# Two input rows per partition moved from Pool's load to SyncE's load at the start of a mixture-of-experts kernel

## The chip, the cores and the metric

The kernel runs on one core of one Trainium2 chip. The metric is device time in microseconds (us) of that core for one execution. The kernel before takes 180.09 us, the median of three runs (179.96 to 180.34).

A core has five instruction streams that concern us: TensorE (PE in the profile, its weight loads PEld), VectorE (DVE), ScalarE (ACT), GpSimd (POOL, called Pool here) and SyncE (SP). Loads and stores between the chip's memory (HBM) and the on-chip memory (SBUF) are carried by 16 DMA engines. A transfer is issued by Pool or by SyncE, is cut into packets, and is spread over all 16 DMA engines. In the profile q0 is the queue of what Pool issues and q1 of what SyncE issues. Only what Pool issues changes the type of the numbers on the way here (float32 in HBM to bfloat16 in SBUF); SyncE's load keeps float32.

## What is computed

```python
n_experts, capacity, hidden, expert_hidden = 8, 256, 512, 2048
# x  (8, 256, 512)   w1 (8, 512, 2048)   w2 (8, 2048, 512), all float32
h = np.matmul(x, w1)
h = np.maximum(h, 0)
return np.matmul(h, w2).astype(np.float32)
```

For each of eight experts, 256 tokens go through two matrix products with a ReLU between. x has 4 MB, the weights 64 MB together, the output 4 MB.

## The kernel before

**Memory.** All places in SBUF are given by hand. `w1_sb` and `w2_sb` have four slots (NS), one expert each, in bfloat16. `hT` holds the hidden layer of one expert, `xT` the transposed x of all experts, `out_sb` the output of all experts in float32. Two of these places have a second use at the start: `x_sb`, the x in bfloat16, is slot 2 of `w2_sb` (line 73), and `x_head`, the float32 copy of the first rows of x, lies in the places of the first experts of `out_sb` (line 134).

**x.** The 2,048 rows of x are laid out as 128 partitions of R = 16 rows with 512 numbers each; a partition's 16 rows lie side by side in HBM (`x_v`, line 49). The first HEAD rows of each partition are loaded by SyncE in float32 into `x_head` (line 136), before the two calls that close the setup (lines 138 and 139), and VectorE casts them into `x_sb` (line 215) once they have landed (semaphore `d_head`). The rest is loaded and cast on the way by Pool (line 154), as its first instruction after the setup. TensorE's transposes (line 329) wait for the cast (`s_cast`), for the identity matrix that Pool makes (lines 155 to 166), and for Pool's load (`d_pool`). They take four rounds of 16; VectorE and ScalarE copy the results from PSUM to `xT` (line 207).

**Weights.** Pool issues all weight loads (line 191), in the order of the list `loads` (lines 119 to 125): w1 of experts 0 and 1, w2 of the same two, then w1 and w2 of 2 and 3, then 4 and 5, then one expert at a time, the last w2 in two halves. The first three are issued without a wait, right after the identity. The w2 load of experts 2 and 3 waits for the transposes, since it overwrites `x_sb`; the later ones wait until the expert that had the slot before is done. SyncE waits for each load's landing and passes it on to TensorE as a count (line 144).

**Experts.** TensorE runs a loop of eight experts. For each, 64 matmuls (two halves of 32, a loop of its own) make the hidden layer in `h_ps`; ScalarE applies the ReLU and writes `hT` (line 240). Then 32 matmuls make the output in `o_ps`, which VectorE copies to `out_sb` (line 226), and ScalarE for the very last half expert (line 246).

**Stores.** Pool stores experts 0 to 6 in one transfer (line 194), issued behind all loads; SyncE stores expert 7 (line 146) when its copies are done. A tiny store ahead of the last weight load (line 182) takes part in the order of the two.

Of the kernel before, what the change touches and what calls it, by code (L numbers as in the profile page):

```python
# [16 lines left out]
def kernel(  # L17
# [14 lines left out]

    R = E * C // P

    HEAD = 4

    NS = 4

# [94 lines left out]

    x_head = out_sb[:, :HEAD // MC].rearrange("p e m h -> p (e m h)")

    head = nc.sync.dma_start(x_head, x_v[:, :HEAD * H]).then_inc(d_head, 16)
    tc.info.no_tile_sem_insts.add(head.ins.name)
# [15 lines left out]
    pool = nc.gpsimd  # L153
    pool.dma_start(x_sb[:, HEAD * H:], x_v[:, HEAD * H:]).then_inc(d_pool, 16)  # L154
    pool.memset(identity[:], 0.0).then_inc(s_event)  # L155
# [58 lines left out]
    dve.wait_ge(d_head, 16)  # L214
    dve.tensor_copy(x_sb[:, :HEAD * H], x_head).then_inc(s_cast)  # L215
    dve.sem_inc(c_xt[0], 1)
# [259 lines left out]
```

## Time and profile before

| | |
|---|---|
| median of three runs | 180.09 us |
| the profiled execution's own time | 179.48 us |
| its span, first to last instruction | 178.2 us |
| mean granted TensorE clock, share of full speed | 0.939 |
| DMA packets, bytes written | 3744, 40.37 MB |
| SyncE's load of the head of x, issue at 0.74 us | 1024 KB, 4.7 us to landing |
| Pool's load of the rest of x, issue at 2.41 us | 1536 KB (as written), 10.8 us to landing |

All figures but the first come from one profiled execution; the profile's own times count from the start of its span. Bytes of a DMA are counted as they are written: a load that turns float32 into bfloat16 reads twice what is counted, so 212 GB/s of it is 424 GB/s of HBM reads. "Share" of a DMA queue is the time of its packets over the time of 16 DMA engines, so in a stretch of T us with n packets the mean packet took share x 16 x T / n; packets are picked by their start, so the share of a short stretch can be far over 100%. In the DMA line of the page a digit is the busy share of a fortieth of the span in tenths. Rows of a timeline read: start, duration, engine, line, operation, written tile <- read tile, and in brackets how long the engine had been idle and what released it.

### The profile page before, as it was taken

Reading aid. Unit: us, or ns where it says so; the run is one execution under the profiler, and the core shown is the slowest. Engines: PE = TensorE matmul, PEld = TensorE weight load, DVE = VectorE, ACT = ScalarE, POOL = GpSimd, SP = SyncE. Lnnn points to the kernel's source line nnn. Section 1 sums busy time; section 2 is a strip of 40 time slices with the busy share of each in tenths; the row PEclk is TensorE's granted clock in tenths of the full one; section 3 lists DMA queues with packets and bytes.
Section 4 is the critical chain, followed back from the end, with each engine's and each line's share of the span. In section 5 each row is a group of like instructions: output and inputs, shape, how many; then the busy total and the mean of one; then the engine's idle time right before and its main releaser. Section 6 shows DMA issues by size and latency. Waiting matters only on the chain. (4 is left out here: it accounts for less than half of the span.)

```text
span 178.2 us, 2068 instructions
## 1 busy us (share of the span) xinstructions
PE 128.2 (72%) x824; PEld 90.4 (51%) x832; DVE 15.8 (9%) x20; ACT 38.7 (22%) x38; POOL 10.9 (6%) x21
## 2 busy tenths in 40 slices
PE   0007620694029999996059999999999999949991
PEld 0006520593013596495024794695696597438740
DVE  0203420000000110020000200200200110020001
ACT  2002420044000044045000152062044044004401
POOL 4500010000000002011000101100020000001000
PEclk9999999999755999999858999999999999996998
DMA  6999999999999999999999999999999999999997
GB/s 208 240 203 232 224 202 221 224 217 206 228 217 202 232 217 199 232 221 195 232 224 195 232 224 199 224 224 202 221 224 217 206 228 213 206 206 221 294 424 326
DMA packets 3744, 40.37 MB, mean 227 GB/s; under 512 B 288, under 2 KB 288, under 8 KB 1312
## 3 DMA queue, kind: packets, MB, share of 16 engines
q0 software_dynamic: 3456, 38.80, 97.7%
q1 hardware_dynamic: 288, 1.57, 2.4%
HBM read 71.30 MB, written 4.20 MB: 424 GB/s over the span
## 5 line engine op out<-in xcount | busy, mean ns | idle before, releaser
L276 PE MATMUL o_ps<-w_sb,hT 128*128 x248 | 60.5, 399 | 18.7 <-PEq L99 17.9
L276 PE MATMUL h_ps<-xT,w_sb 128*128 x512 | 61.8, 284 | 11.5 <-PEq L99 11.5
L276 PEld LDWEIGHTS h_ps<-xT,w_sb 128*128 x512 | 58.3, 146 | 15.9 <-issue 12.2
L240 ACT ACTIVATE hT<-h_ps 128x1024 bf16<-128x1024 f32 x32 | 32.8, 1024 | 111.1 <-PE h_ps L276 111.1
L276 PEld LDWEIGHTS o_ps<-w_sb,hT 128*128 128x128 bf16 x256 | 25.5, 102 | 50.9 <-issue 24.7
L226 DVE COPY out_sb<-o_ps 128x512 f32<-128x512 f32 x15 | 9.7, 687 | 141.2 <-PE o_ps L276 141.2
L276 PE MATMUL xt_ps<-identity,w_sb 128*128 128x128 bf16 x64 | 7.6, 310 | 15.9 <-PEq L99 15.9
L276 PEld LDWEIGHTS xt_ps<-identity,w_sb 128*128 x64 | 6.5, 145 | 16.7 <-issue 16.7
L191 POOL DMA_DIRECT2D w_sb<-in_w_dram x12 | 8.1, 673 | 103.5 <-PE h_ps L276 57.8
L207 ACT COPY xT<-xt_ps 128x1024 bf16<-128x1024 bf16 x4 | 4.0, 1012 | 17.2 <-PE xt_ps L276 17.2
L207 DVE COPY xT<-xt_ps 128x1024 bf16<-128x1024 bf16 x4 | 4.9, 1225 | 12.3 <-PE xt_ps L276 12.3
L194 POOL DMA_DIRECT2D out_dram<-out_sb x1 | 1.0, 964 | 33.5 <-DMA out_dram<-out_sb 33.5
L246 ACT COPY out_sb<-o_ps 128x512 f32<-128x512 f32 x1 | 0.6, 586 | 5.9 <-PE o_ps L276 5.9
L207 ACT ACT_TABLE_LOAD x1 | 1.3, 1283 | 2.0 <-PEq L139 2.0
L215 DVE CAST w_sb<-out_sb 128x2048 bf16<-128x2048 f32 x1 | 1.2, 1227 | 5.5 <-DMA out_sb<-in_x_dram 5.5
L182 POOL DMA_DIRECT2D out_dram<-out_sb x1 | 0.5, 512 | 14.7 <-DVEq L229 14.7
L154 POOL DMA_DIRECT2D w_sb<-in_x_dram x1 | 0.7, 682 | 2.0 <-POOLq L139 2.0
L158 POOL TENSOR_SCALAR_AFFINE_SELECT identity<-identity 128x128 bf16<-128x128 bf16 x1 | 0.3, 284 | 0.2 <-POOL identity L155 0.2
L155 POOL MEMSET identity<- 128x128 bf16 x1 | 0.2, 224 | 0.0
L460 POOL MEMSET const-float32-0.0<- 128x1 f32 x1 | 0.1, 94 | 0.2 <-issue 0.2
L460 POOL MEMSET const-bfloat16-1.0<- 128x1 bf16 x1 | 0.1, 97 | 0.0
L460 POOL MEMSET const-uint8-127<- 128x1 uint8 x1 | 0.1, 97 | 0.0
(1 smaller groups left out, 0.1 us busy)
## 6 DMA issues: line engine op xcount, KB each, us to landing
w_sb<-in_w_dram POOLq DMA_DIRECT2D x5, 4096.0 KB, 47.1
w_sb<-in_w_dram POOLq DMA_DIRECT2D x5, 2048.0 KB, 51.1
out_dram<-out_sb POOLq DMA_DIRECT2D x1, 3584.0 KB, 12.9
w_sb<-in_w_dram POOLq DMA_DIRECT2D x2, 1024.0 KB, 43.6
w_sb<-in_x_dram POOLq DMA_DIRECT2D x1, 1536.0 KB, 10.8
out_sb<-in_x_dram SPq DMA_DIRECT2D x1, 1024.0 KB, 4.7
out_dram<-out_sb SPq DMA_DIRECT2D x1, 512.0 KB, 3.1
out_dram<-out_sb POOLq DMA_DIRECT2D x1, 1.0 KB, 33.9
```

The lines of the kernel that those rows point to most:

```text
L154: pool.dma_start(x_sb[:, HEAD * H:], x_v[:, HEAD * H:]).then_inc(d_pool, 16)
L158: pool.affine_select(out=identity[:], in_=identity[:], compare_op=mybir.AluOpType.not_equal, fill=1.0, base=0, pattern=[[-1, P]], channel_ ...
L182: pool.dma_start(out_v[:16, 0, :16], out_sb[:16, 0, 0, :16]).then_inc(d_pool, 16)
L191: pool.dma_start(dst, src).then_inc(landed[i][0], 16)
L194: pool.dma_start(out_v[:, :E - 1, :], out_sb[:, :E - 1].rearrange("p e m h -> p e (m h)")).then_inc(d_pool, 16)
L207: return copy(xT[:, ko, m].rearrange("k (ep r2) -> k ep r2", r2=R // MC), xt_ps[m][:].rearrange("k r2 ep -> k ep r2"),)
L215: dve.tensor_copy(x_sb[:, :HEAD * H], x_head).then_inc(s_cast)
L226: cp = dve.tensor_copy(out_sb[:, e, m, :], o_ps[m][:])
L240: act.activation(hT[:, g * GJ:(g + 1) * GJ, :].rearrange("p a c -> p (a c)"), h_ps[g % UG][:], mybir.ActivationFunctionType.Relu,).then_in ...
L246: act.copy(out_sb[:, E - 1, 1, :], o_ps[1][:]).then_inc(v_last)
L276: return pe.add_instruction(inst)
L460: nc = _bacc.Bacc("TRN2", target_bir_lowering=False, num_devices=1)
```

## The change

SyncE's load takes six of the sixteen rows of each partition instead of four, Pool's takes ten instead of twelve. `HEAD` appears in the shape of `x_head` (two experts' places of `out_sb` become three), in both loads, and in VectorE's cast of the head, which becomes 128 x 3072 instead of 128 x 2048. No instruction is added, removed or moved in any engine's stream.

```diff
@@ -32,7 +32,7 @@
 
     R = E * C // P
 
-    HEAD = 4
+    HEAD = 6
 
     NS = 4
 
```

The lines that use it, unchanged:

```python
x_head = out_sb[:, :HEAD // MC].rearrange("p e m h -> p (e m h)")
head = nc.sync.dma_start(x_head, x_v[:, :HEAD * H]).then_inc(d_head, 16)
...
pool.dma_start(x_sb[:, HEAD * H:], x_v[:, HEAD * H:]).then_inc(d_pool, 16)
...
dve.tensor_copy(x_sb[:, :HEAD * H], x_head).then_inc(s_cast)
```

## The prediction

> **What bounds the kernel now.** I read the page's DMA lines first, then the chain of waits, then the waits of SyncE's queue.
>
> ```profile
> PE 128.2 (72%) x824; PEld 90.4 (51%) x832; DVE 15.8 (9%) x20; ACT 38.7 (22%) x38; POOL 10.9 (6%) x21
> DMA  6999999999999999999999999999999999999997
> q0 software_dynamic: 3456, 38.80, 97.7%
> q1 hardware_dynamic: 288, 1.57, 2.4%
> HBM read 71.30 MB, written 4.20 MB: 424 GB/s over the span
> ```
>
> The 16 DMA engines are full from the first slice to the last; TensorE is busy 72% and waits for weights. q0 is Pool's queue, q1 SyncE's. The chain that ended last agrees, once its start is asked about:
>
> ```profile
> 158.49 0.04 issue
> 158.53 8.85 PE h_ps L276 x64
> ...
> 174.37 0.59 ACT out_sb L246
> ```
> ```profile
> SPq L144 <- DMA w_sb<-in_w_dram: 166.0, 12, 30.7
> ```
>
> SyncE waits 166.0 us for weights. The chain starts at 158.53, when the last expert's w1 has landed, and runs on TensorE to the last store. That store does not find the DMA engines idle either (by stretches: length, busy time of PE, PEld, DVE, ACT, POOL, clock, DMA share, GB/s):
>
> ```profile
> 172.00:174.00 2.00, 2.00 (x11) 0.87 (x9) 0.00 (x0) 0.00 (x0) 0.00 (x0) 1.00 1.02 422
> 174.00:176.00 2.00, 0.34 (x2) 0.00 (x0) 0.69 (x1) 0.59 (x1) 0.00 (x0) 1.00 1.01 414
> 177.00:178.20 1.20, 0.00 (x0) 0.00 (x0) 0.00 (x0) 0.00 (x0) 0.00 (x0) 0.50 0.18 72
> ```
>
> So the end is the end of a packet stream that has no holes. Each DMA engine carries its own sixteenth of every load, and a load has landed when the last engine is through. The next four rows are the DMA view by the start of packets (queue: packets, MB, time of these packets as a share of 16 engines over the stretch), for 20 to 140 us, 7.5 to 12 us, 12.095 to 12.100 and 12.911 to 12.915:
>
> ```profile
> q0 software_dynamic: 1713, 25.97, 101.4%
> ...
> q0 software_dynamic: 80, 0.98, 103.0%
> ...
> q0 software_dynamic: 1, 0.02, 1532.5%
> ...
> q0 software_dynamic: 1, 0.02, 1915.6%
> ```
>
> First row: 1.014 x 16 x 120 / 1713 = 1.136 us for 15.16 kB, which is 1.228 us for a weight packet of 16,384 B; a single one (third row) took 15.325 x 16 x 0.005 = 1.226 us. For 120 us, then, no packet was slow, whatever the engines did. The third and fourth rows are the first weight packet on the quickest and on the slowest DMA engine: 12.10 and 12.91. With equal work and no slow packets behind, these 0.8 us must still stand when the last w1 lands. **What the slowest DMA engine loses before 12.9 us is paid at the end of the kernel, one for one; nothing else in the first 13 us is.** That is where the change works.
>
> **The change part by part.** The stretch before 13 us, from the timeline:
>
> ```profile
> 0.74 0.38 SPq L136 DMA_DIRECT2D out_sb<-in_x_dram  x1
> 2.41 0.68 POOL L154 DMA_DIRECT2D w_sb<-in_x_dram  x1 [1.96 <-POOLq L139]
> 3.99 2.85 POOL L191 DMA_DIRECT2D w_sb<-in_w_dram  x3 [0.15 <-issue]
> 5.46 1.23 DVE L215 CAST w_sb<-out_sb 128x2048 bf16<-128x2048 f32 x1 [5.46 <-DMA out_sb<-in_x_dram]
> 13.73 1.89 PE L276 MATMUL xt_ps<-identity,w_sb 128*128 128x128 bf16 x16 [13.73 <-PEq L99]
> ```
>
> *The bytes.* From 3.25 to 4.60 only the head moves:
>
> ```profile
> q1 hardware_dynamic: 70, 0.57, 100.2%
> ```
>
> That is 1.002 x 16 x 1.35 / 70 = 0.309 us for a head packet of 8,192 B. A packet of Pool's x load (24,576 B read, 12,288 written) took 1.030 x 16 x 4.5 / 80 = 0.927 us between 7.5 and 12. Per byte read both are 0.0377 us/kB. Each DMA engine has 8 of each. After: 8 head packets of 12,288 B at 0.309 x 1.5 = 0.464, and 8 of Pool's reading 20,480 B at 0.927 x 5/6 = 0.772. Before 8 x (0.309 + 0.927) = 9.89 us, after 8 x (0.464 + 0.772) = 9.89. Moving rows between the queues is worth 0.00 by itself: 1.24 us more head, 1.24 us less rest.
>
> *The cast L215.* 1.23 x 1.5 = 1.84 us, starting 1.24 us later, at 6.7, done by 8.5. Its reader is PE at 13.73, which also waits for the whole of x. Cost nothing, with 5 us of cover; beyond that the transposes would be late, whose result is first used when the first weight load has landed, 28.5 us after its issue at 3.99 (next rows). TensorE's, ScalarE's and SyncE's other work is the same.
>
> *SyncE's and Pool's issues.* One instruction each, as before, for 128 rows:
>
> ```profile
> w_sb<-in_x_dram POOLq DMA_DIRECT2D x1, 1536.0 KB, 10.8
> out_sb<-in_x_dram SPq DMA_DIRECT2D x1, 1024.0 KB, 4.7
> ```
>
> x is complete at 2.41 + 10.8 = 13.2, the head at 5.4. Pool's three weight issues follow: 2.85 us in all, minimum, median and maximum (ns), and the times from issue to landing, in the view of this line for that stretch:
>
> ```profile
> L191 POOL DMA_DIRECT2D w_sb<-in_w_dram x3: 733/748/1383, 4.0 to 5.4; - x3
> ...
> DMA to landing us min/median/max: 28.5/47.1/65.8
> ```
>
> The 1383 is the third, from 5.45, and the cast stands over it from 5.46 to 6.69; the first two took 733 and 748. After the change the cast starts at 6.7, when three issues of 0.74 from 3.99 are over (6.2). Pool would gain 0.64 us, but the third load stands behind the second, which lands at 4.73 + 47.1 = 51.8: worth nothing through Pool's own order.
>
> The Trainium skill (SBUF — State Buffer, "SBUF: two separate sides") says that a VectorE fp32 copy from SBUF to SBUF holds a port that GpSimd needs to write descriptors, and that the DMA engines then wait for these. The long third issue agrees; by this rule the sum would be 0 if x's own descriptors had been written by 5.46, and a gain of the kind worked out next if not.
>
> *The take-over from head to rest.* Here is the one loss that the change can touch. Pool's packets that start between 4.62 and 7.5:
>
> ```profile
> q0 software_dynamic: 48, 0.59, 102.6%
> ```
>
> 1.026 x 16 x 2.88 / 48 = 0.985 us, against 0.927 afterwards: 0.058 x 3 packets = 0.17 us lost on an average engine. On the slowest one it is more. Its first two packets start at 5.104 and 6.276 (asked for in the stretches 5.104 to 5.105 and 6.276 to 6.277); six normal ones follow, up to 12.9:
>
> ```profile
> q0 software_dynamic: 1, 0.01, 7443.8%
> ...
> q0 software_dynamic: 1, 0.01, 7450.0%
> ```
>
> They took 74.438 x 16 x 0.001 = 1.191 and 1.192 us: 2 x 0.265 = **0.53 us lost**. These slow packets lie where Pool issues (3.99 to 6.84) and where the cast runs (5.46 to 6.69). No head packet between 3.25 and 4.6 was slow, although Pool was issuing from 3.99. After the change that stretch carries head packets until 5.86 to 6.34, and Pool's first packets meet at most the last 0.3 us of Pool's issuing. Bounds: all of it goes, -0.53; nothing goes, 0; with the cast as its cause it grows, +0.26 to +0.53 (below). I take -0.45, nearer to the first, since the row of head packets is clean beside the same issuing.
>
> *The start.* Packets started from 1.70 to 3.25, and the first two of the slowest engine (from 1.855 to 1.865 and from 2.390 to 2.395):
>
> ```profile
> q1 hardware_dynamic: 49, 0.40, 93.4%
> ...
> q1 hardware_dynamic: 1, 0.01, 331.9%
> ...
> q1 hardware_dynamic: 1, 0.01, 710.0%
> ```
>
> Mean 0.934 x 16 x 1.55 / 49 = 0.473 us against 0.309; the two took 0.531 and 0.568, so 0.48 lost. If this is a slow stretch of time, the larger packets lose the same: 0. If each early packet takes longer in proportion, 1.5 x 0.48 = 0.72: +0.24. I take 0, because full speed is there by 3.25 on all engines, which began up to 0.7 us apart.
>
> Sum: 0.00 (bytes) + 0 (cast) + 0 (issues) - 0.45 (take-over) + 0 (start) = -0.45 us. The profiled execution took 179.48 us, its span 178.2 and 1.3 around it, 0.61 below the median 180.09. Taken off the profiled 179.48 that gives 179.03; as a difference it holds for the median too: **179.65 us**, own range 179.45 to 179.9. About 0.36 us (0.2%) is what a measurement of this kernel can tell from no change.
>
> **The rivals.**
>
> *Nothing changes (180.1).* The slow packets belong to the beginning of Pool's queue, whenever that is; then they move 1.24 us later with it. For: they are the first and second of Pool's. Against: most engines' first Pool packet was not slow (average loss 0.17, slowest 0.53). It also comes out so if Pool's packets now alternate with the head's: the same bytes on the same engines; the head then lands later, within the cast's 5 us. The Trainium skill (DMA: Bandwidth & Descriptors, "Issuing engines are not separate DMA queues") says that transfers of all issuers run on the same 16 engines, so spreading them saves issue time only; the equal 0.0377 us/kB agree, and by that rule alone it is this case.
>
> *Slower: the cast is what slows Pool's packets (180.35 to 180.6).* Place: L215, now 1.84 us long and over Pool's packets from beginning to end, where the old one met two per engine. Price: 0.265 us for each packet touched. 1.84 us over packets of 0.77 touch three or four: 3 x 0.265 - 0.53 = +0.26, or 4 x 0.265 - 0.53 = +0.53. It decides from four packets on the slowest engine. For: the two slow packets (5.10 to 7.47) enclose the cast. Against: the row for 20 to 140 us has VectorE copying beside unslowed packets, though from PSUM.
>
> *Slower start (180.1 + 0.24 = 180.33)*, as worked out above, with the take-over's loss unchanged. For: two early packets in a row were slow. Against: from 3.25 on no head packet is slow on any engine.
>
> *The change doesn't do what it says:* the issue row of either load would still show 1024 and 1536 KB. An edit of two row counts leaves no room for it; no chance given.
>
> **How the numbers follow.** Take-over loss gone: 0.50 (0.40 beyond 0.36 us, 0.10 within). Nothing changes: 0.20 (0.02 faster, 0.16 within, 0.02 slower). Cast: 0.20 (0.02 within, 0.18 slower, being the higher price or the lower with some of the start's). Start: 0.10 (0.06 within, 0.04 slower). So faster 0.42, same 0.34, slower 0.24. The range runs from all of the 0.53 gone and a little jitter (179.45) to the cast's upper price (180.65).
>
> **What would show it.** Bytes: SyncE's head 1536 KB, landing near 6.6; Pool's rest 1280 KB, x complete near 12.7 instead of 13.2. Cast: about 1.84 us from 6.7. Issues: three at L191 of about 0.75 us each. Take-over: the mean Pool packet from 5.9 to 8.5 at 0.77 us, not 0.80 or more, and the last engine's first weight packet at 12.4. PE's start on the last expert and the span then come 0.4 to 0.5 us earlier. Wrong: slow packets under the new cast (12.91 rises to 13.2), slow ones at the start of Pool's queue again (12.91 stays), or an end that does not follow the first weight packet of the slowest engine.

## The result and the profile after

| | before | after |
|---|---|---|
| median of six runs each | 179.95 us | 179.25 us |
| lowest to highest | 179.68 to 180.34 | 179.17 to 179.49 |
| ratio after / before, 95% interval | | 0.9961 [0.9948, 0.9974] |
| profiled execution, its own time / span | 179.48 / 178.2 us | 179.49 / 178.2 us |

The change makes the kernel 0.70 us faster, which is more than the predicted 0.45 and below the predicted range. Yet the two profiled executions are equally long. Both statements are true, and the second one is where a reader of a single profile goes wrong here.

The timeline and the issue rows of the kernel after, beside those shown of before:

```profile
3.98 2.19 POOL L191 DMA_DIRECT2D w_sb<-in_w_dram  x3 [0.15 <-issue]
7.21 1.76 DVE L215 CAST w_sb<-out_sb 128x3072 bf16<-128x3072 f32 x1 [7.21 <-DMA out_sb<-in_x_dram]
```
```profile
out_sb<-in_x_dram SPq DMA_DIRECT2D x1, 1536.0 KB, 6.4
w_sb<-in_x_dram POOLq DMA_DIRECT2D x1, 1280.0 KB, 10.8
```

The bytes moved as the diff says; Pool's three issues take 0.66 us less than before (2.19 for 2.85), since the cast no longer stands over the third. But the head lands at 0.74 + 6.4 = 7.1 us and x is complete at 2.40 + 10.8 = 13.2, where the prediction had 6.6 and 12.7; the reason follows. Now the DMA view of the kernel after by the start of packets (queue: packets, MB, share of 16 engines), for 5.9 to 8.5 us, for 2.015 to 2.016, and for 12.931 to 12.932:

```profile
q0 software_dynamic: 54, 0.55, 101.5%
q1 hardware_dynamic: 21, 0.06, 5.9%
...
q1 hardware_dynamic: 1, 0.01, 10087.5%
...
q0 software_dynamic: 1, 0.02, 7662.5%
```

First row: 1.015 x 16 x 2.6 / 54 = 0.782 us for a Pool packet, against 0.772 worked out without any loss: the take-over from head to rest is clean. Third row: one of the first head packets took 100.875 x 16 x 0.001 = 1.614 us, where 0.464 is normal. That DMA engine is the slowest of this execution, and its first weight packet starts at 12.93 (last row), against 12.91 before. The take-over's 0.53 us was saved and 1.15 us was lost at the start, in this one execution. (In these traces the next packet of a busy DMA engine starts within some 30 ns of the end of its last one, so the packets can be followed engine by engine. The slowest engine of before began at 2.39 us, 0.37 us later than this one, and lost 0.26 us in its first packet and 0.53 at the take-over: 1.16 us together, as much as the 1.15 here.) The end follows:

```profile
158.53 0.04 issue
158.57 8.87 PE h_ps L276 x64
```

TensorE begins the last expert at 158.57; before it was 158.53. So the page of after shows no gain, because the profiled execution is the slowest of its six runs (179.49), and that of before was faster than all six of its own (179.48 against 179.68 and more).

### The profile page after: what moved, and what is told of

It reads as the page before. It is cut to its first block, busy times and chain, and to the rows that moved or that the text cites. A ratio compares the mean times of both kernels' runs of the same rounds, so it can differ in the third digit from the quotient of the medians.

```text
span 178.2 us, 2076 instructions
## 1 busy us (share of the span) xinstructions
PE 127.1 (71%) x832; PEld 89.6 (50%) x832; DVE 16.4 (9%) x20; ACT 38.7 (22%) x38; POOL 10.2 (6%) x21
## 5 line engine op out<-in xcount | busy, mean ns | idle before, releaser
L276 PE MATMUL o_ps<-w_sb,hT 128*128 x256 | 59.8, 394 | 19.5 <-PEq L99 19.5
L191 POOL DMA_DIRECT2D w_sb<-in_w_dram x12 | 7.4, 618 | 103.4 <-PE h_ps L276 57.1
L215 DVE CAST w_sb<-out_sb 128x3072 bf16<-128x3072 f32 x1 | 1.8, 1760 | 7.2 <-DMA out_sb<-in_x_dram 7.2
## 6 DMA issues: line engine op xcount, KB each, us to landing
w_sb<-in_x_dram POOLq DMA_DIRECT2D x1, 1280.0 KB, 10.8
```

What stands on the lines that cost most here:

```text
L191: pool.dma_start(dst, src).then_inc(landed[i][0], 16)
L276: return pe.add_instruction(inst)
```

## The experiments

Sixteen runs were made in four groups (e1 to e4, e5 to e8, e9 to e12, e13 to e16), each group beside the kernel before on the same chip; e4 and e12 repeat the change and the kernel before. "Take-over" is the time at which a DMA engine has finished its share of the head and turns to Pool's queue.

### Is it the cast, or Pool's issuing?

**e1_cast_on_scalar** (HEAD 4, the cast moved to ScalarE)

```diff
-    dve.wait_ge(d_head, 16)
-    dve.tensor_copy(x_sb[:, :HEAD * H], x_head).then_inc(s_cast)
+    act.wait_ge(d_head, 16)
+    act.copy(x_sb[:, :HEAD * H], x_head).then_inc(s_cast)
```

> HEAD stays 4; the cast of the head runs on ScalarE instead of VectorE, at the same time. Theory 1 (the VectorE cast beside Pool's third weight issue is what slows Pool's first packets): the third issue takes 0.73 to 0.75 us instead of 1.38, Pool's x packets all take about 0.93 us, and the time falls by 0.4 to 0.7 us, as with the change. Theory 2 (Pool's queue is slow at its beginning as long as Pool issues, whatever is cast): slow packets of 1.05 to 1.3 us stay, the time stays within 0.2 us of before. Theory 3 (any cast that reads and writes SBUF beside the packets slows them): slow packets stay and last longer, as ScalarE's cast is longer.

Measured 180.29 against 180.18 us, ratio 0.9998 [0.9977, 1.002]. Pool's third issue is back at 0.73 us, but nothing is gained. The view of the issue line, and two answers of the DMA view for 5.214 to 5.483 and 5.483 to 5.484:

```profile
L191 POOL DMA_DIRECT2D w_sb<-in_w_dram x3: 728/733/746, 4.0 to 5.4; - x3
```
```profile
q1 hardware_dynamic: 1, 0.00, 0.2%
...
q0 software_dynamic: 1, 0.01, 12918.8%
```

A DMA engine ended the head at 5.21; no data packet started anywhere until 5.48, and the one that starts then took 129.188 x 16 x 0.001 = 2.07 us instead of 0.93. The loss is larger than in the profiled execution of before, with no VectorE cast beside it. So VectorE's cast is not needed for it; Pool's issuing is still in question.

**e2_cast_late** (HEAD 4, VectorE's cast waits for all of x)

```diff
     dve.wait_ge(d_head, 16)
+    dve.wait_ge(d_pool, 16)
```

> HEAD stays 4; VectorE's cast waits for the whole of x (about 13.2 us), so that it meets neither Pool's issues nor x's packets. Theories 1 and 3: no slow Pool packet before 8 us, 0.4 to 0.7 us faster than before; the later start of the transposes (by about 1.2 us) costs nothing, since the first weights land at 32 us. Theory 2: slow packets stay, no change. If the transposes were on the path it would be about 1 us slower.

180.28 against 180.18 us, ratio 0.9999 [0.9977, 1.0021]. The cast ran at 14.55, and from 5.767 to 5.768 the DMA view has a Pool packet of 118.812 x 16 x 0.001 = 1.90 us:

```profile
q0 software_dynamic: 1, 0.01, 11881.2%
```

No cast of any engine is needed for the loss. The later transposes cost nothing that shows in the time, as expected.

**e3_issue_under_cast** (HEAD 6, Pool's third weight issue waits for the head)

```diff
+        if i == 2:
+            pool.wait_ge(d_head, 16)
         pool.dma_start(dst, src).then_inc(landed[i][0], 16)
```

> HEAD is 6 as in the change; Pool's third weight issue waits until the head has landed, so that it stands under the cast again (from about 7 us). Theory 1: the third issue takes over 1.3 us again and some Pool packets between 7 and 9 us take 0.1 to 0.4 us more than the 0.775 of the change; the gain of the change is lost in part or whole (0.2 to 0.7 us slower than the change). Theories 2 and 3: like the change, all Pool packets 0.78 to 0.80 us, -0.7 us to before.

179.18 us, ratio 0.9939 [0.9918, 0.9959]: like the change. The timeline has the third issue under the cast, 1.64 us long:

```profile
7.06 1.64 POOL L193 DMA_DIRECT2D w_sb<-in_w_dram  x1 [1.60 <-DMA out_sb<-in_x_dram]
```

So the cast does hold up Pool's issue, and it costs nothing, as the prediction had it for that load. It does not slow the packets: those of Pool that start under it, from 6.79 to 8.55, take 1.273 x 16 x 1.76 / 46 = 0.779 us each.

```profile
q0 software_dynamic: 46, 0.47, 127.3%
```

**e4_after_again** (the change once more)

> The change itself once more, for a second trace and a tighter ratio. All theories: 0.5 to 0.8 us faster than before (ratio 0.996 to 0.997), no slow Pool packet. If the slow first head packet of the first trace (its slowest DMA engine lost 1.15 us on its first packet) is chance, the first weight packet of the slowest engine starts at 12.5 to 12.7 here instead of 12.93; if it belongs to the larger head packets, it is at 12.9 again.

179.19 us, ratio 0.995 [0.9928, 0.9972]. The slowest engine's first weight packet starts at 12.43, so the 12.93 of the first trace was chance of its start. Yet this execution took 179.45 us, as long as the first one: weight packets later on were slow in it, which the part on the prediction comes back to.

**e5_issues_after_cast** (HEAD 4, Pool issues no weights until the cast has ended)

```diff
+        if i == 0:
+            pool.wait_ge(s_cast, 1)
         pool.dma_start(dst, src).then_inc(landed[i][0], 16)
```

> HEAD is 4; Pool's weight issues wait for the cast of the head, so Pool issues nothing from 3.9 to about 6.7 us, when its x packets begin (4.6 to 5.3). Theory R1 (a DMA engine's first Pool packets are held up because Pool is writing and announcing further loads at that time): no slow packet and no idle 0.3 us at the take-over, the gain of the change (0.7 to 1.0 us) is there with HEAD 4. Theory R2 (Pool's queue is taken up too soon after its x issue, whatever Pool does next): slow packets of 1.1 to 2.1 us stay, time as before.

180.2 against 180.32 us, ratio 1.0001 [0.9977, 1.0025]. Pool issues nothing between 3.8 and 7.0, and a packet that starts between 5.218 and 5.219 takes 1.49 us:

```profile
q0 software_dynamic: 1, 0.01, 9300.0%
```

**e6_issues_at_takeover** (HEAD 6, five small memsets of an unused place ahead of the weight issues)

```diff
+        if i == 0:
+            for k in range(5):
+                pool.memset(spare[:, k], 0.0)
         pool.dma_start(dst, src).then_inc(landed[i][0], 16)
```

> HEAD is 6; five small memsets of an unused place hold Pool's first weight issue back by about 1.1 us, so that the three issues stand over the take-over again (about 5.1 to 7.3 us, take-over 6.0 to 6.5). R1: one DMA engine or more has a first or second Pool packet of over 1 us instead of 0.78, and 0.4 to 1.0 us of the gain is lost. R2: like the change.

179.17 us, ratio 0.995 [0.9933, 0.9967]. The memsets were shorter than I had reckoned, but the issues, from 4.51 to 6.70, still stand over the take-over (6.0 to 6.6). Timeline, then Pool packets from 5.9 to 8.5:

```profile
4.51 2.19 POOL L195 DMA_DIRECT2D w_sb<-in_w_dram  x3
```
```profile
q0 software_dynamic: 54, 0.55, 102.1%
```

That is 0.787 us each: clean. Pool's issuing is not the cause either, in both directions.

### Is it the time since Pool's issue of x?

What is left to test is that at 4.6 to 5.2 us Pool's queue was not yet ready for the DMA engines.

**e7_x_after_identity** (HEAD 6, x issued after the identity)

```diff
-    pool.dma_start(x_sb[:, HEAD * H:], x_v[:, HEAD * H:]).then_inc(d_pool, 16)
     pool.memset(identity[:], 0.0).then_inc(s_event)
...
     ).then_inc(s_event)
+    pool.dma_start(x_sb[:, HEAD * H:], x_v[:, HEAD * H:]).then_inc(d_pool, 16)
```

> HEAD is 6; Pool makes the identity first and issues its load of x after it (from about 3.4 instead of 2.4 us), the weight issues right behind. R2: the time from x's issue to the take-over is nearly as short as with HEAD 4, so slow first packets are back in part and some of the gain is lost. R1: the first weight issue still ends before the take-over, the second and third reach into it a little more than with the change (about 0.1 us later), so like the change or nearly.

179.21 us, ratio 0.9945 [0.9927, 0.9964]. The issue moved by 0.4 us only (2.84 to 3.52), so the take-over is still 2.4 us behind it. It settles nothing between the two theories.

**e8_head8** (`HEAD = 8`)

> HEAD is 8 instead of 6: take-over near 7.4 us, after all of Pool's issues. R1 and R2: no slow packet, same time as the change within 0.3 us (ratio to before 0.994 to 0.996), since with 6 the take-over was already clean. If more head helps by itself (fewer bytes through Pool's queue), it is another 0.4 us or more faster.

179.23 us, ratio 0.9953 [0.9935, 0.9971]: no better than 6. Once the take-over is late enough, more head gives nothing.

**e9_x_early_head4** (HEAD 4, Pool's x issued before the setup is closed)

```diff
     tc.info.no_tile_sem_insts.add(head.ins.name)
+    rest = nc.gpsimd.dma_start(x_sb[:, HEAD * H:], x_v[:, HEAD * H:]).then_inc(d_pool, 16)
+    tc.info.no_tile_sem_insts.add(rest.ins.name)
...
-    pool.dma_start(x_sb[:, HEAD * H:], x_v[:, HEAD * H:]).then_inc(d_pool, 16)
```

> HEAD is 4; Pool's load of x is issued before the setup is closed, near 0.8 instead of 2.4 us, everything else as before. Theory R2 (a DMA engine that turns to Pool's queue less than about 2.4 us after the end of Pool's x issue finds it not ready in full: idle 0.3 us, slow first packets): the take-over at 4.6 to 5.2 us is now 3 us after the issue, so no slow first Pool packet, and 0.7 to 1.0 us faster than before with HEAD 4. Theory R3 (it is the larger head or its larger packets that help, not the time since Pool's issue): slow packets stay, time as before within 0.3 us.

184.09 us, ratio 1.0218 [1.0194, 1.0241]: a miss as a kernel, because the closing of the setup now waits until x has landed and Pool's weight issues come at 14.90 instead of 3.99. Its packets still answer the question. Timeline, then Pool's packets started from 4.55 to 7.5:

```profile
1.23 0.68 POOL L138 DMA_DIRECT2D w_sb<-in_x_dram  x1 [0.79 <-PEq L141]
...
14.90 2.19 POOL L192 DMA_DIRECT2D w_sb<-in_w_dram  x3
```
```profile
q0 software_dynamic: 49, 0.60, 96.2%
```

0.962 x 16 x 2.95 / 49 = 0.927 us: HEAD 4 and no slow packet, with the x issue 1.2 us earlier. (Nor was Pool issuing anything else then; e5 showed that this alone does not help.) It is not quite clean: one DMA engine, whose head ended at 4.77, started its first Pool packet only at 5.23, 3.3 us behind the end of the issue.

The same trace shows the start of Pool's queue a second time, with no other queue beside it. The first weight issue ends near 15.6; the first weight packets of the 16 engines start from 16.36 to 17.16 and take 1.970 x 16 x 0.9 / 16 = 1.77 us instead of 1.23 (DMA view, 16.3 to 17.2):

```profile
q0 software_dynamic: 16, 0.26, 197.0%
```

**e10_x_late_head6** (HEAD 6, 14 memsets ahead of the x issue; e13 has 21 and e14 has 29)

```diff
+    for k in range(14):
+        pool.memset(spare[:, k], 0.0)
     pool.dma_start(x_sb[:, HEAD * H:], x_v[:, HEAD * H:]).then_inc(d_pool, 16)
```

> HEAD is 6; 14 small memsets hold Pool's load of x back to about 3.8 us, end of issue about 4.5, so that the take-over at 6.0 to 6.5 comes 1.5 to 2 us behind it, as with HEAD 4. R2: slow first Pool packets (1.0 us and more instead of 0.78) on several DMA engines again, and 0.4 to 1.0 us of the change's gain lost. R3: like the change.

179.29 us, ratio 0.9948 [0.9928, 0.9968]. The issue ended at 4.56, 1.5 to 1.8 us ahead of the take-over. The 16 first Pool packets, from 6.02 to 6.40:

```profile
q0 software_dynamic: 16, 0.16, 222.6%
```

2.226 x 16 x 0.38 / 16 = 0.846 us, so 0.07 too long on average: slow packets are back, but small, and no measurable part of the gain is lost. Neither theory had this.

**e11_head2** (`HEAD = 2`)

> HEAD is 2: the head would be through at 3.3 to 4 us, 0.2 to 0.9 us after Pool's x issue ends. R2: the DMA engines stand idle or slow longer than with 4, 0.5 to 2 us slower than before. R3: slower than before by about as much as 6 is faster than 4, 0.7 to 1.0 us, without idle time at the take-over.

181.13 us, ratio 1.0051 [1.003, 1.0071]. From 3.34 to 3.79 us head packets started and none of Pool's; the first 16 of Pool's follow from 3.79 to 5.40, with a mean of 1.024 x 1.61 = 1.65 us, against 1.08 for those behind. (Fifteen of them are the first on their engine; the sixteenth engine starts its first at 5.67.) The stretch view shows how few packets start then (second to last column their share, last GB/s). It counts packets by their start, so it does not say that the engines stand more than half of the time: long packets from before 4.50 are still under way on most of them, and three engines have had none of Pool's until 5.26, 5.32 and 5.67.

```profile
q1 hardware_dynamic: 34, 0.09, 50.1%
...
q0 software_dynamic: 16, 0.23, 102.4%
```
```profile
4.50:5.50 1.00, 0.00 (x0) 0.00 (x0) 0.72 (x1) 0.00 (x0) 1.00 (x3) 1.00 0.45 72
```

Pool's issue of x ended at 3.09. So Pool's queue comes into use on one DMA engine after the other, 0.7 to 2.6 us behind the end of the issue. HEAD 4 turns to it 1.5 to 2.2 us behind, in the last part of that time; HEAD 6 at 2.9 and later.

**e12_before_again** (the kernel before)

> The kernel before once more, for a second trace. All theories: time as before. If the profiled execution of before was a mild one (179.48 against a median of about 180.1 us), the slowest DMA engine's first weight packet starts later than its 12.91 us here, at 13.0 to 14 us, with a take-over loss of 0.7 to 1.5 us on that engine instead of 0.53.

180.44 us, ratio 1.0015 [0.9996, 1.0033]. The first weight packet of its slowest engine started at 13.08; that engine stood 0.11 us and then had Pool packets of 1.35 and 1.04 us, about 0.65 us lost at the take-over, a little under what was expected. The profiled execution, 179.92 us, was again a fast one, the fastest of its ten.

**e13_x_later_head6 and e14_x_latest_head6** (as e10, with 21 and 29 memsets)

> HEAD is 6; 21 memsets hold Pool's load of x back to 4.6 us, end of issue 5.3, so the take-over at 6.0 to 6.5 comes about 0.7 to 1.2 us behind it (1.5 to 2.2 with HEAD 4, 0.3 to 1.0 with HEAD 2). R2 (Pool's queue becomes ready engine by engine some 0.7 to 2.4 us behind the end of the x issue, and whoever turns to it earlier waits): idle gaps at the take-over and first Pool packets of 1 to 2 us, 0.4 to 1.0 us slower than the change. R3 (the size of the head alone counts): like the change.

> HEAD is 6; 29 memsets hold Pool's load of x back to 5.5 us, end of issue 6.1, at the take-over itself, as with HEAD 2. R2: gaps of 0.5 to 2 us on all DMA engines and slow first packets, 1.5 to 2.5 us slower than the change. R3: a gap only until Pool's first descriptors are there, under 1 us.

181.47 us, ratio 1.0062 [1.0037, 1.0087], and 181.32 us, ratio 1.0053 [1.0035, 1.007]: slower than before, and 2.3 and 2.1 us slower than the change, whose sizes they have. Stretches of after, of e13 and of e14, in this order:

```profile
6.70:7.40 0.70, 0.00 (x0) 0.00 (x0) 0.19 (x1) 0.00 (x0) 0.00 (x0) 1.00 1.11 234
```
```profile
5.50:6.00 0.50, 0.00 (x0) 0.00 (x0) 0.00 (x0) 0.00 (x0) 0.27 (x2) 1.00 0.92 393
...
6.70:7.40 0.70, 0.00 (x0) 0.00 (x0) 0.52 (x1) 0.00 (x0) 0.70 (x2) 1.00 0.50 59
```
```profile
6.00:6.70 0.70, 0.00 (x0) 0.00 (x0) 0.00 (x0) 0.00 (x0) 0.70 (x3) 1.00 0.10 35
6.70:7.40 0.70, 0.00 (x0) 0.00 (x0) 0.52 (x1) 0.00 (x0) 0.46 (x2) 1.00 0.27 29
```

From 6.70 to 7.40 packets of 234 GB/s start in the change, of 59 in e13 and of 29 in e14. Pool's issue ended at 5.55 in e13 and at 6.67 in e14. In e14 the engines stand: the last head packet ends at 6.52, and all 16 first Pool packets start between 7.38 and 8.10, again 0.7 to 1.4 us behind the end of the issue. In e13 they stand in part and are slow in part: the first Pool packets start from 6.30 to 7.58, up to 1.6 us behind the end of that engine's head, and those that start from 6.30 to 6.91 take 2.072 x 16 x 0.61 / 14 = 1.44 us instead of 0.78:

```profile
q0 software_dynamic: 14, 0.14, 207.2%
```

In e14 the cast begins 0.2 us behind the issue, so some of its gap may be the cast's; in e13 the cast begins 1.3 us behind.

**e15_table_late** (HEAD 6, ScalarE's table load waits for the head)

```diff
     act = nc.scalar
+    act.wait_ge(d_head, 16)
     act.sem_inc(c_xt[1], 1)
```

> HEAD is 6; ScalarE's table load, which stands over the slow start of the head (2.0 to 3.3 us), waits until the head has landed. If the table load is what makes the first head packets slow (0.9 to 1.2 us instead of 0.46): they become normal and the time falls by another 0.3 to 0.6 us below the change. If it is the start of the transfers itself: like the change within 0.15 us.

179.18 us, ratio 0.9934 [0.9908, 0.996]: like the change. Head packets started from 1.70 to 3.25 took 0.993 x 16 x 1.55 / 32 = 0.770 us with the table load gone to 6.83, and 0.917 x 24.8 / 30 = 0.758 in after. The table load is not what makes them slow. Rows of e15 and of after:

```profile
q1 hardware_dynamic: 32, 0.39, 99.3%
```
```profile
q1 hardware_dynamic: 30, 0.37, 91.7%
```

**e16_extra_load** (HEAD 4, SyncE loads two rows of x a second time into an unused place)

```diff
     tc.info.no_tile_sem_insts.add(head.ins.name)
+    extra = nc.sync.dma_start(
+        out_sb[:, 2].rearrange("p m h -> p (m h)"), x_v[:, HEAD * H:(HEAD + 2) * H]
+    ).then_inc(d_head, 16)
+    tc.info.no_tile_sem_insts.add(extra.ins.name)
...
-    dve.wait_ge(d_head, 16)
+    dve.wait_ge(d_head, 32)
```

> HEAD is 4 and Pool's load keeps its twelve rows; SyncE loads two rows of x a second time into an unused place behind the head, so that the take-over comes at 6.0 to 6.5 us as with the change, and 1.24 us of DMA time are added. R2: first Pool packets all about 0.93 to 0.95 us, no gap; against before the loss of the take-over is saved (0.7 to 1.0) and 1.24 paid: 0.2 to 0.55 us slower than before. R3 (what helps is that Pool's load is smaller or the head's packets larger): the loss stays, 1.2 us slower than before.

180.33 against 180.36 us, ratio 0.9994 [0.9975, 1.0014]. 1.24 us more to load cost nothing, which means that about 1.2 us were saved. Against the change (179.2 us in the other groups), whose take-over is as late, it is 1.1 us slower, about the price of the extra load. The x issue ran from 2.88 to 3.56 here, the take-over came 2.4 us and more behind it, and Pool's twelve rows came in 1.072 x 16 x 2.6 / 48 = 0.929 us a packet (5.9 to 8.5):

```profile
q0 software_dynamic: 48, 0.59, 107.2%
```

The runs of e16 lie between 180.20 and 180.46 but for one of 181.23, those of before between 179.29 and 181.21: with the take-over late, most of the scatter goes too. (The 181.23 is the profiled execution; its slowest first weight packet starts at 13.71, and weight packets later on were slow.) So the time that passes before the DMA engines turn to Pool's queue is enough without the smaller rest and the larger head packets (e16), and these are not enough without the time (e13, e14).

## Why the prediction came out as it did

**Right in part: what sets the end.** "What the slowest DMA engine loses before 12.9 us is paid at the end of the kernel, one for one." The test is the time of the profiled execution less the start of the slowest engine's first weight packet. It is 166.55 to 166.58 in seven traces: before (12.91 and 179.48), after (12.93 and 179.49), e3, e7 (12.58 and 179.16), e8, e14 (14.79 and 181.34) and e15 (12.48 and 179.06). There the statement holds, over 2.3 us. In the other eleven it is 0.2 to 0.95 us more, from 166.75 (e11) to 167.52 (e16); e4 has 167.02 and e12 has 166.84. In each of these eleven some weight packets took longer than normal, which none did in the seven. Rows of e6 (167.44) and of before, 60 to 70 us, where all packets are weights:

```profile
q0 software_dynamic: 128, 2.10, 100.9%
```
```profile
q0 software_dynamic: 129, 2.11, 98.9%
```

That is 1.009 x 160 / 128 = 1.261 us a packet against 0.989 x 160 / 129 = 1.227. The prediction had read from the one trace of before that no packet is slow behind 20 us. What is lost there is lost with either size of the head, and what causes it was not looked for.

**Right: bytes, cast, issues.** A clean Pool packet took 0.782 us (worked out: 0.772); the cast took 1.76 us (1.84) and hid; Pool's shorter third issue was worth nothing (e1, e3).

**Right: the start, though one row was read wrongly.** It was taken as 0 with +0.24 as the other bound. The two packets of 0.531 and 0.568 us are not of one engine: behind the one that starts at 1.859 its engine's next starts at 2.386, and the slowest engine's first packet is that of 2.39. It lost 0.26 us there, not 0.48, and the other bound by the same sum would have been +0.13. Head packets before 3.25 us lose (0.758 - 0.463) x 30 / 16 = 0.55 us an engine after and (0.473 - 0.309) x 49 / 16 = 0.50 before. On one engine it can be much more, and was in the profiled execution (1.15 us).

**Right in its direction, wrong in its size and its reason: the take-over.** This is the step that failed. I took 0.45 of the 0.53 us that the slowest DMA engine lost there. The 0.53 came from one profiled execution, which was a mild one; single early Pool packets of 1.49, 1.90 and 2.07 us in other executions with HEAD 4 (e5, e2, e1) lose 0.6 to 1.1 us each, and more with the idle time ahead of them. What is saved on average is what the medians say, 0.70 us in the first comparison and 0.99 in the second (180.18 to 179.19). The traces agree: the slowest engine's first weight packet starts at 12.91, 13.08, 13.15, 13.90 and 14.19 in the five with HEAD 4 and the early take-over (before, e12, e5, e1, e2), and from 12.43 to 12.93, with a median of 12.55, in six with HEAD 6 and the late one (after, e3, e4, e6, e7, e15). The medians are 0.6 us apart, the means 0.8. I wrote the bound "all of it goes, -0.53" as if the trace held the most that can be lost, and set the range's lower end by it. The trace gave one draw of a quantity that is a maximum over 16 engines.

The reason was wrong too. I put the slow packets down to Pool's issuing and the cast beside them; e1, e2 and e5 took these away and kept the loss, e3 and e6 brought them back and lost nothing. The rival "nothing changes", that the slow packets belong to the beginning of Pool's queue, was nearer in what it blamed, but had the queue's trouble move with the take-over. That both queues take the same time for a byte would by itself have left the time as it was; it fell by 0.70 us. The trouble stays with the issue: the first Pool packets come 0.7 to 2.6 us behind the end of Pool's instruction, engine by engine, and those drawn within that time are often slow; a longer head covers it (e11, e13, e14, e16).

**Wrong: the cast as what slows packets.** e2 and e3 leave nothing of this rival.

**Open.** e10, with the same 1.5 to 1.8 us behind the issue as the kernel before, lost only some 0.1 us. The time since the issue therefore does not tell the whole amount; what makes the last part of the wait shorter there was not found. The two kernels differ in the sizes of head and rest, so at this distance the sizes may matter after all. In e9, on the other hand, one engine got its first Pool packet 3.3 us behind the issue. How much of the 0.7 to 1.0 us belongs to slow weight packets, which can differ between the runs of two kernels, was not separated either; e16, with HEAD 4, a late take-over and little scatter, speaks for the take-over. What the DMA engines lack in that time is also not shown: the traces have packets only, not what is queued. The slow start of the head itself (0.5 us an engine, the largest loss that remains) is not ScalarE's table load; its cause was not looked for further.

## What to carry to other kernels

When a kernel is one unbroken stream of packets, look at the moments at which the DMA engines change from one queue to another, and let the first queue's work last until the second is ready: here some 2.4 us between the end of Pool's issue and its first packet were enough in e7 and e16, and beyond the change's six rows more head (e8) gave nothing. A loss that is the worst of 16 engines differs from execution to execution, so its size is to be read from several traces or from the scatter of the times; a single profile gives the place, not the price. Moving work is cheap to test by adding some: e16 paid 1.24 us and got it back.

## What was not expected

Up to HEAD 6 the DMA engines finished all head packets before they took one of Pool's. With HEAD 8 (e8) they did not. DMA view, 6.7 to 8.5 us:

```profile
q0 software_dynamic: 32, 0.26, 69.6%
q1 hardware_dynamic: 16, 0.26, 34.7%
```

The 16 engines started 32 packets of Pool's and 16 head packets in that stretch, and the cast, which waits for the whole head, began at 9.36 us. It cost nothing here, since x is needed only as a whole, but a head that something waits for would have come late.

The scatter of the times is part of the gain. In the second group the kernel before ran from 179.22 to 181.24 us in 34 runs, and the kernels with a late take-over (e6, e7, e8) from 179.10 to 179.60 in 34 of 36; the other two, both of e6, took 179.69 and 180.12.
